# Three column tiles beside the arriving input, a fourth under the norm, and the shift from two more context columns

## Chip, cores and metric

One core of a Trainium2 chip runs the whole kernel. The metric is device time in microseconds (us) from start to end of one execution; several executions were timed, and one more was taken with the profiler. Engines: PE multiplies matrices, PEld loads its weights, DVE, ACT and POOL work on elements, SP issues most of the DMAs.

## What is computed

The kernel is one layer of a diffusion backbone over 1024 latent tokens of width 1024, with 256 context tokens in front. Cut to what matters here:

```python
u_lat = _modulate(_rmsnorm(x, norm1_g[l]), sh1, sc1)        # x*(1+scale)+shift
u_ctx = _modulate(_rmsnorm(ctx, norm1_g[l]), csh1, csc1)
rgx_l, rgg_l, mlx_l, mlo_l, gr_l, gm_l = jnp.split(u_lat @ w_in, splits, axis=-1)
rgx_c, rgg_c, mlx_c, mlo_c, gr_c, gm_c = jnp.split(u_ctx @ w_in, splits, axis=-1)
...
xm_l, q_l, k_l, v_l, gin_l = _mlstm_inputs(_to_col_major(mlx_l, rows), ml_conv_w, ml_conv_b, ml_wq, ml_wk, ml_wv)
...
y_lat = _merge(y_rg_l, y_ml_l, gr_l, gm_l, w_branch_rg, w_branch_ml, w_out)
x = x + g1 * y_lat
h = _modulate(_rmsnorm(x, norm2_g[l]), sh2, sc2)
x = x + g2 * _swiglu(h, w_ffn_in[l], w_ffn_out[l])
```

The scales and shifts are products of a small vector with `w_mod`. The change touches the norm, the modulation, and the first column tiles of `u @ w_in` (those of `mlx`, numbers 16 to 23 of `w_in`). It rests on this: with x, the norm's factor r per token, the scale a per channel and the shift s per channel, `(x*a*r + s) @ W` is `r * ((x*a) @ W) + s @ W`. So a tile can be multiplied before r is known; its output is multiplied by r afterwards, and one number per output channel, the shift term `s @ W`, is added.

## The kernel before

**Numbers in two halves.** Each operand of a matmul is a rounded high half and a low half (the rest). `load_split` (L89) loads a tile of weights (128x1024) into `wr`, POOL makes the high half `wh` (L94), DVE the low half `wl` (L97). `gemm` (L104) runs three products per 128-deep step k, each as a pair of 512-wide matmuls: high by high (L110), low of the input by high (L112), high by low of the weights (L114). One column tile against one k is called a part: six matmuls. A tile is eight parts.

**The beginning** (L338 to L454) is written out by hand: PE, ACT, DVE and POOL take their instructions in the order of the text. The input comes in eight pieces x[k]; a wmod pair (`mod_a` L276, `mod_b` L288) gives the scale of two pieces: PE forms `psmod`, ACT copies it to `mo`, PE sums it with `sel` to `psm`, DVE adds it into `modc` and `a1`. `un_h` (L315) is ACT's scaled copy, the high half of the input without the norm; `un_lo` (L319) DVE's low half; `un_sq` (L322) ACT's square, summed on DVE for the norm. `part(k, (0, 1))` multiplies tiles 16 and 17 with piece k; the scaled copy of piece k+1 stands ahead of part k in the text.

**The norm.** `rms_cols` (L140) sums the squares over the partitions (`prms`) and takes the root, `bcast_col` (L148) spreads the result over the partitions through PE (`rbl`), ACT copies it to `rb`. Meanwhile the last shift products (`mod_a`, `mod_b` of 0 to 3) and the shift term are formed: `psh` (L411), 16 products of a whole weight tile with one column. Then x is loaded again, `normed` (L328) and `normed_low` (L333) write the real modulated input into `uh` and `ul` in the order KB, beginning with piece 5, and tiles 18 and 19 are multiplied piece by piece with it. Beside this ACT squares the context pieces and POOL sums them (L307), and POOL multiplies the outputs X of tiles 16 and 17 by `rb` (L445).

**The stage behind it** (pool `p1`, L458 on, ordered by the scheduler) forms small matrices (`small_mats` L476), and for each of the eight tiles the context columns (`context` L495, 256 wide), for tiles 20 to 23 the latent ones (`latent` L490), then a convolution, a tanh and the small products `pv` and `pgt`. Then come an RG-LRU part whose first gate matmuls are `pt` (L700), and the mLSTM: `gate_out(4)` (L806) multiplies four column tiles of the output gates, which need nothing of the mLSTM, and then `head` (L817) runs four times. Head 0 loads masks and G, its inputs `xa`, `vv` and two matrices of decay rows, `SW` and `Sb`, each in two directions, by SP's queue; its first matmul is `pq` (L842).

## Time and profile before

| | |
|---|---|
| median of three runs | 1912.44 us (1911.99 to 1913.51) |
| the profiled execution's own time | 1913.69 us |
| its span | 1911.9 us |
| mean granted clock of PE | 0.991 of full speed |
| PE busy | 1847.2 us, 97% of the span |
| DVE, ACT, POOL busy | 64%, 32%, 18% |
| chain of waits that ended last | PE 89%, DVE 6%, ACT, DMA, POOL and issue 1% each |

The rows below are of that execution; times in them are us from the start of its span. A row of a timeline gives the start, the duration (of all its instructions together), engine, line, operation, tiles and count, and in brackets how long the engine stood idle before it and what released it.

### The profile page before, as it was taken

What the parts mean: (1) busy time and instruction counts of PE and PEld (TensorE: products, weight loads), DVE (VectorE), ACT (ScalarE), POOL (GpSimd) and SP (SyncE); (2) the same over time, 40 slices, a digit from 0 to 9 for tenths busy, and PEclk for the clock granted to TensorE, in tenths of its full rate; (3) what the DMA queues carried; (4) which work ended last, traced back from release to release, by engine and by line L of the source; (5) the groups of instructions that cost most, each with busy time, mean ns of one, the idle gap of its engine ahead of it and who ended that gap; (6) DMA issues with size and microseconds to landing.
All of it is one profiled execution on the core that took longest, in us unless ns stands there. A gap on an engine that the chain in (4) does not pass through costs nothing.

```text
span 1911.9 us, 23058 instructions
## 1 busy us (share of the span) xinstructions
PE 1847.2 (97%) x8878; PEld 1520.5 (80%) x8878; DVE 1230.9 (64%) x1887; ACT 610.0 (32%) x842; POOL 348.0 (18%) x452
## 2 busy tenths in 40 slices
PE   6799999999999999999999999999999999999997
PEld 4678778888877878788888888778888888888886
DVE  4676558888716474747776446787755555587755
ACT  3433256767422222222310112443333333210013
POOL 0311111111116151515101013220000000110003
PEclk9899999999999999999999999999999999999998
DMA  9432211212260515150796444343322222653102
GB/s 269 153 141 114 91 53 51 65 50 68 100 187 21 166 25 163 26 162 13 253 346 236 145 150 140 105 143 133 132 85 86 78 83 100 222 176 107 56 1 88
DMA packets 89989, 228.83 MB, mean 120 GB/s; under 512 B 8056, under 2 KB 37272, under 8 KB 89752
## 3 DMA queue, kind: packets, MB, share of 16 engines
q1 hardware_dynamic: 77160, 183.28, 30.0%
q0 software_dynamic: 11888, 43.54, 5.9%
q8 instruction: 70, 1.15, 0.3%
q10 hardware_dynamic: 832, 0.53, 0.1%
q14 instruction: 39, 0.32, 0.1%
HBM read 177.42 MB, written 49.91 MB: 119 GB/s over the span
## 4 chain that ended last, share of the span: by engine, by line
PE 89%; DVE 6%; ACT 1%; DMA 1%; issue 1%; POOL 1%; SPq 0%; DVEq 0%; ACTq 0%
PE pg L110 11%; PE pg L112 11%; PE pg L114 11%; PE pp L1122 7%; PE pp L1124 7%; PE pp L1123 7%; PE pp L1334 4%; PE pp L1336 4%; PE pp L1335 4%; PE po L891 3%; PE pC L896 3%; PE po L889 2%; PE po L110 2%; PE po L112 2%; PE po L114 2%; DMA wm<-in_wmod 1%
## 5 line engine op out<-in xcount | busy, mean ns | idle before, releaser
L110 PE MATMUL pg<-ah,wh 128*128 128x512 f32 x896 | 284.6, 398 | 4.6 <-ACT X L222 3.5
L112 PE MATMUL pg<-al,wh 128*128 128x512 f32 x896 | 282.7, 396 | 5.4 <-DVE al L335 5.4
L114 PE MATMUL pg<-ah,wl 128*128 128x512 f32 x896 | 280.6, 394 | 1.6 <-DVE wl L97 1.6
L94 POOL TENSOR_SCALAR wh<-wr 128x1024 fp32r<-128x1024 f32 x102 | 114.3, 1124 | 597.2 <-PE pg L112 217.5
L97 DVE TENSOR_TENSOR wl<-wr,wh 128x1024 fp32r<-128x1024 f32 x102 | 126.6, 1243 | 120.1 <-POOL wh L94 119.5
L112 PEld LDWEIGHTS pg<-al,wh 128*128 128x128 f32 x896 | 165.4, 190 | 39.9 <-DVE al L335 6.2
L110 PEld LDWEIGHTS pg<-ah,wh 128*128 128x128 f32 x896 | 165.4, 191 | 37.9 <-issue 5.6
L114 PEld LDWEIGHTS pg<-ah,wl 128*128 128x128 f32 x896 | 165.7, 189 | 36.9 <-DVE wl L97 2.0
L1334 PE MATMUL pp<-hh,wh 128*128 128x512 f32 (+1 forms) x384 | 145.1, 378 | 0.0
L1336 PE MATMUL pp<-hh,wl 128*128 128x512 f32 (+1 forms) x384 | 144.8, 377 | 0.0
L1335 PE MATMUL pp<-hh,wh 128*128 128x512 f32 (+1 forms) x384 | 144.8, 377 | 0.0
L1348 DVE SCALAR_TENSOR_TENSOR xs<-pp,g,xs 128x512 f32<-128x512 f32 x144 | 105.3, 746 | 47.8 <-PE pp L1336 43.9
L1122 PE MATMUL pp<-th,oh 128*128 128x512 f32 x264 | 102.8, 389 | 0.0
L1124 PE MATMUL pp<-th,ol 128*128 128x512 f32 x264 | 102.7, 389 | 0.0
L1123 PE MATMUL pp<-tl,oh 128*128 128x512 f32 x264 | 102.7, 389 | 0.0
L1134 DVE TENSOR_TENSOR c<-c,pp 128x512 f32<-128x512 f32 x82 | 56.2, 685 | 69.7 <-PE pp L1124 53.0
L1163 ACT ACTIVATE oh<-os 128x512 fp32r<-128x512 f32 x88 | 55.4, 631 | 130.9 <-PE pp L1123 111.7
L1282 POOL DMA_DIRECT2D s_h<-c x44 | 24.0, 545 | 356.6 <-DVE c L1281 356.6
L1164 DVE TENSOR_TENSOR ol<-os,oh 128x512 fp32r<-128x512 f32 x88 | 60.5, 689 | 39.8 <-ACT oh L1163 39.8
L1334 PEld LDWEIGHTS pp<-hh,wh 128*128 128x128 f32 x384 | 73.1, 190 | 14.0
L1335 PEld LDWEIGHTS pp<-hh,wh 128*128 128x128 f32 x384 | 73.0, 190 | 14.1
L1336 PEld LDWEIGHTS pp<-hh,wl 128*128 128x128 f32 x384 | 73.0, 190 | 13.8
(337 smaller groups left out, 3811.8 us busy)
## 6 DMA issues: line engine op xcount, KB each, us to landing
wr<-in_wfi SPq DMA_DIRECT2D x52, 512.0 KB, 3.3
wr<-in_win SPq DMA_DIRECT2D x48, 512.0 KB, 3.4
wr<-in_wmt SPq DMA_DIRECT2D x32, 512.0 KB, 5.1
s_h<-c POOLq DMA_DIRECT2D x44, 256.0 KB, 2.6
wr<-in_wfo SPq DMA_DIRECT2D x22, 512.0 KB, 3.9
g<-s_h SPq DMA_DIRECT2D x22, 512.0 KB, 4.6
wm<-in_wmod SPq DMA_DIRECT2D x16, 512.0 KB, 6.8
wr<-in_wo SPq DMA_DIRECT2D x16, 512.0 KB, 3.5
```

The lines of the kernel that those rows point to most:

```text
L94: nc.gpsimd.tensor_scalar(h, r, 1.0, 0.0, op0=ALU.mult, op1=ALU.add)
L97: nc.vector.tensor_tensor(l, r, h.bitcast(F32), op=ALU.subtract)
L110: nc.tensor.matmul(o, lhsT=wh[:, k], rhs=h(k), start=f, stop=False)
L112: nc.tensor.matmul(o, lhsT=wh[:, k], rhs=l(k), start=False, stop=False)
L114: nc.tensor.matmul(o, lhsT=wl[:, k], rhs=h(k), start=False, stop=e)
L1122: nc.tensor.matmul(o, lhsT=wh(k), rhs=bh(k), start=new and k == 0, stop=False, skip_group_check=True)
L1123: nc.tensor.matmul(o, lhsT=wh(k), rhs=bl(k), start=False, stop=False, skip_group_check=True)
L1124: nc.tensor.matmul(o, lhsT=wl(k), rhs=bh(k), start=False, stop=not more and k == n - 1, skip_group_check=True)
L1334: nc.tensor.matmul(po, lhsT=wh[:, m], rhs=hh[:, sl], start=i == 0, stop=False)
L1335: nc.tensor.matmul(po, lhsT=wh[:, m], rhs=hl[:, sl], start=False, stop=False)
L1336: nc.tensor.matmul(po, lhsT=wl[:, m], rhs=hh[:, sl], start=False, stop=i == n - 1)
L1348: nc.vector.scalar_tensor_tensor(xs[:, m, sls[t]], po, g2[:, m:m + 1], xs[:, m, sls[t]], op0=ALU.mult, op1=ALU.add)
```

## The change

Tiles 16, 17 and 18 are multiplied without the norm while the input arrives, 24 parts in place of 16, and `un_h` of a piece stands right ahead of its own part. The second weight tile and the second input piece are loaded ahead of the second wmod pair. Tile 19 is multiplied without the norm too, from the same `uh` and `ul`, while the norm is formed. The loop with the norm then works on tiles 20 and 21. The 16 products `psh` are gone; the context operand gets two more columns that hold the latent shift, so the context matmuls of tiles 16 to 19 are 258 wide and yield the shift term. The four X are multiplied by `rb` on DVE behind the loop (two on POOL in the loop before). The context squares are summed with two wide squares and five POOL additions in place of eight and seven. In `p1` the contexts of six tiles come first, then the small matrices; only tiles 22 and 23 are left for the latent side there; and three of the four gate tiles that stood ahead of the first mLSTM head move into it (`side_early`). PSUM is divided anew, and the scratch for DMA descriptors of POOL's queue shrinks from its default to 4096 bytes.

```diff
+NU = 4
+CW = TC + 2
...
-    ch = uc.tile([128, KT, TC], F32R, name="ch")
-    cl = uc.tile([128, KT, TC], F32R, name="cl")
+    ch_ = uc.tile([128, KT, CW], F32R, name="ch")
+    cl_ = uc.tile([128, KT, CW], F32R, name="cl")
+    ch, cl = ch_[:, :, 0:TC], cl_[:, :, 0:TC]
...
+    xpp = tc.tile_pool(name="xp", bufs=4, reuse_waits="tile")
+    xp = xpp.__enter__()
+    with pool("p0g", bufs=3, space=PSUM) as pg_, pool("p0s", bufs=2, space=PSUM) as ps_:
...
             load_x(0)
-            wfirst = [load_split(win[16], wf_, "f", late=True)]
+            wfirst = [load_split(win[16 + m], wf_, "f", NU, late=True) for m in range(2)]
+            load_x(1)
             load_mod(10, 11)
-            load_x(1)
-            wfirst.append(load_split(win[17], wf_, "f", late=True))
+            wfirst.append(load_split(win[18], wf_, "f", NU, late=True))
...
+            def ctx_sums(j):
+
+                sq = accl.rearrange("p (a b) -> p a b", a=4)
+                nc.scalar.activation(accl, c_t[j].rearrange("p a b -> p (a b)"), AF.Square)
+                nc.gpsimd.tensor_tensor(accl[:, 0:512], accl[:, 0:512], accl[:, 512:1024], op=ALU.add)
+                if j:
+                    nc.gpsimd.tensor_tensor(accc, accc, sq[:, 0], op=ALU.add)
+                    nc.gpsimd.tensor_tensor(accc, accc, sq[:, 1], op=ALU.add)
+                else:
+                    nc.gpsimd.tensor_tensor(accc, sq[:, 0], sq[:, 1], op=ALU.add)
...
             def un_sq(k):
-                sq = accl if k == 0 else (rb, sqx)[k % 2]
+                sq = accl if k == 0 else X4[2 + k % 2][:, 0:T]
                 nc.scalar.activation(sq, x_sb[k], AF.Square)
...
+                first = range(NU - 1)
+                pgs = [pg_.tile([128, 2, 512], F32, tag="g", name="pg") for _ in first]
...
                 un_h(0)
                 wfirst[0][2]()
                 un_lo(0)
-                mod_a(10, 11)
-                load_mod(14, 15)
+                wfirst[1][2]()
+                part(0, (0, 1))
                 un_h(1)
                 un_lo(1)
-                wfirst[1][2]()
+                part(1, (0, 1))
+                mod_a(10, 11)
...
+                wfirst[2][2]()
+                part(0, (2,))
+                mod_b(10, 11)
...
+                part(7, first)
                 mod_b(4, 5, 6, 7)
-                yr = rms_cols(p0, pc_.tile([128, 512], F32, tag="c", name="prms"), accl, 8)
+                put_latent(X4[0], pgs[0])
+                pgs.append(pg_.tile([128, 2, 512], F32, tag="g", name="pg"))
+                yr = rms_cols(p0, ps_.tile([128, 512], F32, tag="s", name="prms"), accl, 8)
...
+                part(KB[0], (3,))
+                part(KB[1], (3,))
                 rbl = [ps_.tile([128, 512], F32, tag="s", name="rbl") for _ in range(2)]
                 for j in range(2):
                     for c in range(4):
                         bcast_col(p0, yr[:, 4 * j + c:4 * j + c + 1], rbl[j][:, c * 128:c * 128 + 128])
                     nc.scalar.activation(rb[:, sls[j]], rbl[j], AF.Copy)
+                    part(KB[2 + j], (3,))
+                wfirst += [load_split(win[16 + m], late=True) for m in (NU, NU + 1)]
...
+                for k in KB[4:]:
+                    part(k, (3,))
...
-                normed(5)
-                psh = ps_.tile([128, 512], F32, tag="s", name="psh")
-                for m in range(2):
-                    for kk in range(KT):
-                        nc.tensor.matmul(psh[:, m:m + 1], lhsT=wfirst[m][3][:, kk], rhs=modc[:, kk, 0:1], start=kk == 0, stop=kk == KT - 1)
-                normed_low(5)
...
                 for i, k in enumerate(KB):
...
-                    if i == 1:
-                        ctx_sums()
-                    if i == 0:
-                        nc.vector.tensor_copy(shw, psh[:, 0:2])
-                    part(k, (2, 3))
-                    if i == 3:
-                        yc = rms_cols(p0, pc_.tile([128, 512], F32, tag="c", name="prms"), accc, 2)
+                    if i in (1, 2):
+                        ctx_sums(i - 1)
+                    part(k, (NU, NU + 1))
+                    if i == 4:
+                        yc = rms_cols(p0, ps_.tile([128, 512], F32, tag="s", name="prms"), accc, 2)
                     if i == 6:
                         rbc = ps_.tile([128, 512], F32, tag="s", name="rbc")
                         for c in range(2):
                             bcast_col(p0, yc[:, c:c + 1], rbc[:, c * 128:c * 128 + 128])
-                    if i in (1, 3):
-                        m = (i - 1) // 2
...
+                sh2 = modc[:, 0:KT, 0:1].to_broadcast([128, KT, 2])
+                nc.scalar.activation(ch_[:, :, TC:CW], sh2, AF.Identity)
+                nc.vector.tensor_tensor(cl_[:, :, TC:CW], sh2, ch_[:, :, TC:CW].bitcast(F32), op=ALU.subtract)
                 for k in range(KT):
                     nc.vector.scalar_tensor_tensor(c_sb[k], c_sb[k], a1[:, k, 1:2], rbc[:, 0:TC], op0=ALU.mult, op1=ALU.mult)
                     nc.scalar.activation(ch[:, k], c_sb[k], AF.Identity, bias=modc[:, k, 1:2])
-                for k in range(KT):
-                    nc.vector.scalar_tensor_tensor(cl[:, k], c_sb[k], modc[:, k, 1:2], ch[:, k].bitcast(F32), op0=ALU.add, op1=ALU.subtract)
-            pgs = pgs[2:]
-
+                    if k:
+                        nc.vector.scalar_tensor_tensor(cl[:, k - 1], c_sb[k - 1], modc[:, k - 1, 1:2], ch[:, k - 1].bitcast(F32),
+                                                       op0=ALU.add, op1=ALU.subtract)
+                k = KT - 1
+                nc.vector.scalar_tensor_tensor(cl[:, k], c_sb[k], modc[:, k, 1:2], ch[:, k].bitcast(F32), op0=ALU.add, op1=ALU.subtract)
+                for X in X4:
+                    xv = X[:, 261:1285].rearrange("p (w r) -> p w r", r=16)
+                    nc.vector.tensor_tensor(xv, xv, rb.rearrange("p (r w) -> p w r", r=16), op=ALU.mult)
...
+            def context(m, X):
+
+                n = CW if m < NU else TC
+                pc = ps_.tile([128, 512], F32, tag="s", name="pc")
+                gemm(wfirst[m], [(pc[:, 0:n], lambda k: ch_[:, k, 0:n], lambda k: cl_[:, k, 0:n])])
+                nc.scalar.activation(X[:, 2:258], pc[:, 0:TC], AF.Copy)
+                if m < NU:
+                    nc.vector.tensor_copy(shw[:, m:m + 1], pc[:, TC:TC + 1])
+                    nc.scalar.activation(X[:, 261:1285], X[:, 261:1285], AF.Identity, bias=shw[:, m:m + 1])
...
+            for m in range(NU):
+                context(m, X4[m])
+            wfp.__exit__(None, None, None)
...
+            def side_early():
+                j, m = sides.pop(0)
+                w = load_split(win[32 + 8 * j + m])
+                pg = pg_.tile([128, 2, 512], F32, tag="g", name="pg")
+                gemm(w, halves(pg, uh, ul))
+                t = wp.tile([128, KT, 128], F32, tag="wr", name="st", bufs=3).rearrange("p a b -> p (a b)")
+                nc.scalar.activation(t, pg.rearrange("p a b -> p (a b)"), AF.Tanh, scale=0.5)
+                nc.gpsimd.dma_start(s_g[j, m], t)
...
             small_mats()
             nc.gpsimd.dma_start(s_G, G)
...
-                    context(m + 1)
+                X = X4[m]
+                if m in (0, 2, 4):
+                    side_early()
+                if m in (4, 5):
+                    latent(m + 2)
...
-        gate_out(4)
+        gate_out(1)
...
-    nc = _bacc.Bacc("TRN2", target_bir_lowering=False, num_devices=1)
+    nc = _bacc.Bacc("TRN2", target_bir_lowering=False, num_devices=1, dynamic_dma_scratch_size=4096)
```

Two places in the order of the instructions. The first is ACT's queue around the third and fourth piece. Before (`ah` is the scaled copy into the high half, `sqx` and `rb` hold squares, `mo` is the copy of a modulation product):

```order
L317 ACTIVATE ah_91<-x_176,a1_73 128x1024
L324 ACTIVATE sqx_150<-x_169 128x1024
L285 ACTIVATE mo_298<-psmod_281 128x256
L317 ACTIVATE ah_91<-x_210,a1_73 128x1024
L324 ACTIVATE rb_152<-x_176 128x1024
L317 ACTIVATE ah_91<-x_212,a1_73 128x1024
```

With the change (`X_149`, `X_150` hold squares):

```order
L318 ACTIVATE ah_91<-x_180,a1_73 128x1024
L284 ACTIVATE mo_332<-psmod_315 128x256
L325 ACTIVATE X_149<-x_180 128x1024
L318 ACTIVATE ah_91<-x_215,a1_73 128x1024
L325 ACTIVATE X_150<-x_215 128x1024
L318 ACTIVATE ah_91<-x_217,a1_73 128x1024
```

Behind the copy of the modulation product the scaled copy came next, and the square after it; now the square comes next, and the scaled copy of piece 3 (`x_215`) after it.

The second place is PE's queue from the sums of the squares (`prms`) to the broadcast of the norm. Before (`pg` are the parts of tiles 16 and 17 with the last piece; `psh` the shift term):

```order
L143 MATMUL prms_476<-ones_70,accl_149 128x1 x8
L110 MATMUL pg_180<-ah_91,wh_162 128x512 x2
L112 MATMUL pg_180<-al_92,wh_162 128x512 x2
L114 MATMUL pg_180<-ah_91,wl_164 128x512 x2
L110 MATMUL pg_181<-ah_91,wh_173 128x512 x2
L112 MATMUL pg_181<-al_92,wh_173 128x512 x2
L114 MATMUL pg_181<-ah_91,wl_175 128x512 x2
L282 MATMUL psmod_516<-wm_431,s2_77 32x128 x8
```

and, after three more `psmod` rows and all but the last of eight `rbl` rows:

```order
L152 MATMUL rbl_556<-dg_579,ones_70 128x128
L292 MATMUL psm_583<-sel_69,mo_549 128x2 x4
L411 MATMUL psh_591<-modc_72,wr_160 128x1 x8
L411 MATMUL psh_591<-modc_72,wr_171 128x1 x8
L110 MATMUL pg_628<-ah_91,wh_366 128x512 x2
L112 MATMUL pg_628<-al_92,wh_366 128x512 x2
L114 MATMUL pg_628<-ah_91,wl_368 128x512 x2
```

With the change (`pg_544` is tile 19 without the norm):

```order
L145 MATMUL prms_545<-ones_70,accl_146 128x1 x8
L112 MATMUL pg_544<-ah_91,wh_418 128x512 x2
L114 MATMUL pg_544<-al_92,wh_418 128x512 x2
L116 MATMUL pg_544<-ah_91,wl_420 128x512 x2
L112 MATMUL pg_544<-ah_91,wh_418 128x512 x2
L114 MATMUL pg_544<-al_92,wh_418 128x512 x2
L116 MATMUL pg_544<-ah_91,wl_420 128x512 x2
L154 MATMUL rbl_580<-dg_582,ones_70 128x128
```

and, after two more `rbl` rows:

```order
L154 MATMUL rbl_580<-dg_591,ones_70 128x128
L112 MATMUL pg_544<-ah_91,wh_418 128x512 x2
L114 MATMUL pg_544<-al_92,wh_418 128x512 x2
L116 MATMUL pg_544<-ah_91,wl_420 128x512 x2
L154 MATMUL rbl_581<-dg_601,ones_70 128x128
```

Parts of a tile that needs no norm now stand between `prms` and the `rbl`, and between the two groups of `rbl`; `psh` is gone, and the products for the shift (`psmod`) stand behind the broadcast.

## Rows read from the trace of the kernel before

**Rows 1.** The page, busy time by engine and its share of the span

```profile
PE 1847.2 (97%) x8878; PEld 1520.5 (80%) x8878; DVE 1230.9 (64%) x1887; ACT 610.0 (32%) x842; POOL 348.0 (18%) x452
```

**Rows 2.** Stages: from:to, length, busy PE, PEld, DVE, ACT, POOL (instructions); PEclk, DMA share, GB/s

```profile
23.45:59.81 36.36, 34.64 (x257) 27.14 (x257) 22.80 (x33) 17.01 (x20) 3.47 (x12) 0.95 0.82 300
59.81:72.10 12.29, 8.43 (x121) 8.12 (x121) 6.05 (x10) 5.37 (x8) 0.00 (x0) 0.87 0.57 189
72.10:105.44 33.34, 27.43 (x105) 21.52 (x105) 25.33 (x30) 15.00 (x24) 14.06 (x9) 0.84 0.22 68
254.64:262.00 7.36, 6.33 (x23) 5.10 (x24) 1.48 (x1) 3.95 (x3) 0.00 (x0) 0.77 0.00 0
```

**Rows 3.** Timeline of PE, 19 to 30 us: start, us, line, operation, count, idle before

```profile
19.73 1.08 PE L282 MATMUL psmod<-wm,s 128*32 128x128 f32 x16 [10.13 <-DMA wm<-in_wmod]
...
25.30 1.05 PE L114 MATMUL pg<-ah,wl 128*128 128x512 f32 x2
26.16 1.05 PE L110 MATMUL pg<-ah,wh 128*128 128x512 f32 x2
...
29.27 0.63 PE L114 MATMUL pg<-ah,wl 128*128 128x512 f32 x2
29.74 0.63 PE L110 MATMUL pg<-ah,wh 128*128 128x512 f32 x2
```

**Rows 4.** Timeline of DVE: first low half of weights; a low half of the input

```profile
19.36 1.23 DVE L97 TENSOR_TENSOR wl<-wr,wh 128x1024 fp32r<-128x1024 f32 x1 [9.37 <-POOL wh L94]
...
44.78 1.28 DVE L320 SCALAR_TENSOR_TENSOR al<-x,a,ah 128x1024 fp32r<-128x1024 f32 x1
```

**Rows 5.** Timeline of ACT: copy of a modulation product, square, scaled copy

```profile
39.67 0.38 ACT L285 ACTIVATE mo<-psmod 128x256 f32<-128x256 f32 x1 [1.91 <-PE psmod L282]
39.95 1.05 ACT L324 ACTIVATE sqx<-x 128x1024 f32<-128x1024 f32 x1
40.90 1.14 ACT L317 ACTIVATE ah<-x,a 128x1024 fp32r<-128x1024 f32 x1
```

**Rows 6.** Timeline of PE, 53 to 96 us

```profile
53.50 2.04 PE L143 MATMUL prms<-ones,accl 128*128 128x1 f32 x16
...
64.89 3.70 PE L411 MATMUL psh<-modc,wr 128*128 128x1 f32 x32 [0.35 <-DVE modc L293]
72.10 1.19 PE L110 MATMUL pg<-ah,wh 128*128 128x512 f32 x2 [3.51 <-ACT X L222]
...
95.01 1.22 PE L112 MATMUL pg<-al,wh 128*128 128x512 f32 x2 [5.38 <-DVE al L335]
```

**Rows 7.** Timeline of POOL, 77 to 93 us

```profile
77.61 7.76 POOL L307 TENSOR_TENSOR accc<-accc,sqc 128x256 f32<-128x256 f32 x7 [18.28 <-ACT sqc L306]
```

**Rows 8.** Groups of DVE lines in the mLSTM: a multiplication through a permuted view

```profile
L954 DVE SCALAR_TENSOR_TENSOR t<-t,y 128x1024 f32<-128x1024 f32 x8 | 15.7, 1960 | 0.2
```

**Rows 9.** Timeline of PE around the first gate matmul

```profile
254.64 0.50 PE L700 MATMUL pt<-xh,rh 128*128 128x512 f32 x1 [2.42 <-ACT xh L666]
256.17 0.50 PE L701 MATMUL pt<-X,rh 128*128 128x512 f32 x1 [1.03 <-DVE X L670]
```

**Rows 10.** Timeline of ACT before it

```profile
245.11 0.39 ACT L657 ACTIVATE X<-pc 128x256 f32<-128x256 f32 x1 [4.04 <-PE pc L114]
```

**Rows 11.** Timeline of SP, loads of the first head

```profile
511.61 0.42 SPq L814 DMA_DIRECT2D masks<-in_masks  x1
...
524.90 1.13 SPq L821 DMA_DIRECT2D xa<-s_xm  x2
...
535.39 4.15 SPq L831 DMA_DIRECT2D SW<-s_row  x1
```

**Rows 12.** Timeline of DVE, masks onto the second decay matrix

```profile
549.81 2.15 DVE L853 TENSOR_TENSOR SW<-SW,masks 128x512 f32<-128x512 f32 x2 [6.93 <-DMA SW<-s_row]
```

**Rows 13.** Timeline of ACT, exponentials of the second decay matrix

```profile
550.53 3.04 ACT L855 ACTIVATE SW<-SW,cols 128x128 f32<-128x128 f32 x10 [4.84 <-DVE SW L853]
```

**Rows 14.** Timeline of PE, first matmul of the first head

```profile
574.13 3.60 PE L842 MATMUL pq<-xa,G 128*128 128x512 f32 x8
```

More of the change, by code (lines that the diff above doesn't have):

```diff
@@ L193, in conv_pads @@
         nc.gpsimd.memset(X[:, 1285:1287], 0.0)
+    sides = [(j, m) for j in range(2) for m in range(KT)]
     uh, ul = act_pool()
@@ L338, in hybrid_block @@
             with tc.manual_schedule(engines=ENG4):
-                pgs = [pg_.tile([128, 2, 512], F32, tag="g", name="pg") for _ in range(2)]
+                first = range(NU - 1)
+                pgs = [pg_.tile([128, 2, 512], F32, tag="g", name="pg") for _ in first]
                 mod_a(8, 9)
@@ L637, in side_store @@
         nc.gpsimd.dma_start(s_g[j, m], side_tanh(pg, t))
-    sides = [(j, m) for j in range(2) for m in range(KT)]
     with pool("p2") as p2, pool("p2c", bufs=1, space=PSUM) as pc_:
```

147 lines of the change are left out of this document (64 added, 83 removed).

## Prediction

> **What bounds the kernel now.** I read the page first: TensorE (PE) is busy 97% of the span [rows 1]. So time can only come from work that PE no longer does, from stretches in which it stands idle, and from stretches at half clock. The change takes almost no work from PE: the 16 products `psh`, 3.70 us [rows 6], and it adds two columns to four context tiles. What it can win is in the idle and slow stretches, so next I read the windows by stage [rows 2]: while the input arrives PE is busy 34.64 of 36.36 us, with the clock at 0.95; in the norm's stage 8.43 of 12.29 us, and none of that is tile work; in the first loop with the norm 27.43 of 33.34 us at 0.84. Then the timeline tells which waits these are: 10.13 us for wmod at the start [rows 3], 3.51 us before the loop and 5.38 us inside it [rows 6], and, later, 2.42 and 1.03 us at the first gate matmul [rows 9].
>
> Prices. Two pairs of matmuls start 0.86 us apart at 25.30 and 0.47 us apart at 29.27 [rows 3]: the half and the full level of the clock. A part has three pairs, so 1.41 us at full clock and 2.58 at half, and a tile of eight parts takes 11.3 us. What a stall costs beyond itself I take from [rows 2], 254.64 to 262.00: the mean clock is 0.77 after the stall of 2.42 us, so 0.23 of 7.36, or 1.7 us, is lost.
>
> The sum goes by five stages; each is compared for the same work of PE, so where the new kernel has done a tile more, 11.3 us are added to the old one.
>
> **A, to the end of the third tile and the sums of squares.** Before: 59.81, and 11.3 for the third tile, 71.1 us. With the change the first pair need not wait for the second wmod pair. The high half of the first weights is there at about 19.4 (its low half begins at 19.36 [rows 4]), 4 us before the old first part at 23.45. From there: 24 parts, 33.8 us; products with wmod, three sets of two at some 1.0 us and one of four at 2.0 (a set took 1.08 at half clock [rows 3]), 5.0 us; the sums with `sel` and `prms` (2.04 at half clock [rows 6]), about 3.9 us as an estimate. Now the waits. The change drops the lead of one piece: the scaled copy of piece 3 stands on ACT behind the copy of the modulation product, which waits for PE, and behind a square. When PE has done that product it therefore waits 0.38 + 1.05 + 1.14 us for the three ACT instructions [rows 5], and after one pair for the rest of the low half on DVE (1.28 us [rows 4] less 0.47): 3.1 us with some overlap taken off. The same pattern is at piece 5. At piece 4 the scale itself comes late, 2.4 us; at piece 2 about 1.0; at piece 0 the low half of the weights and then of the input, 1.23 + 1.28 us less the pairs that run, 1.5. Together 11.1 us, an estimate from walking the queues with these durations. Start at half clock: 1.3 us. Two waits (pieces 3 and 5) are as long as the stall of 2.42, so two more slow stretches, 3.4 us. Sum 19.4 + 33.8 + 5.0 + 3.9 + 11.1 + 1.3 + 3.4 = 77.9, so **+6.8** (+3.5 with no slow stretches, +7.5 if each wait is a little longer).
>
> **B, norm and the loop with the norm.** Before, 59.81 to 105.44: 45.6 us for two tiles, and 11.3 for a third, 56.9. With the change three tiles at full clock take 33.9 us; `rbl` about 1.9, the shift's `psmod` and `psm` 2.7, the sums for the context 1.0, some slow clock behind `prms` 1.4, and waits of 4.6 remain (estimates; the loop still alternates between DVE's two operations and PE). Sum 45.5, **-11.4** (-13 to -9). The low clock, the wait of 3.51 and `psh` go because tile 19 needs nothing of the norm; what covers the norm's chain is its eight parts, 11.3 us against the 12.29 us of the old stage. Without that cover the waits of 3.51 and 5.38 us would be back.
>
> **C, contexts first.** Context 0 now follows the loop at once, paced by two DVE operations per piece that are a quarter as wide as a low half, 0.4 us each as an estimate: 6.4 us for eight pieces against some 3 us of matmuls. Small matrices, which stood there before, no longer fill this. DVE has four multiplications of X ahead of the convolutions, each between 1.28 [rows 4] and 1.96 us [rows 8], where POOL had two. POOL's sums shrink from seven additions (7.76 us [rows 7]) to five, two of them twice as wide, about as long; it was off the path and stays there. **+3** (+2 to +8, the upper end if DVE's four also hold the first convolution up).
>
> **D, before the first gate matmul.** Between the last copy of a context at 245.11 [rows 10] and the first gate matmul at 254.64 [rows 9] lies a chain of copy, convolution and rounding of 9.5 us, and PE ran dry 2.42 us before its end, then waited 1.03 more. In the new order 15 rows of tile work stand there in place of 8: seven more pairs, 3.3 us. That fills the first stall, leaves about 0.7 of both, and the slow stretch of 1.7 goes: **-4.4** (-2 if the slow stretch stays).
>
> **E, the first mLSTM head.** Three gate tiles, 33.9 us, leave their place ahead of head 0 (they fill `p1` instead, where they cost the same). So `pq` comes at 574.13 [rows 14] less 33.9, 540.2. It needs `xa` and G; what follows it, `pS`, needs ACT's copy of it, behind the exponentials of the second decay matrix. Those end 3.7 us after the matrix has landed: 549.81 [rows 12] to 553.6 [rows 13]. Today the landing is 24 us early, afterwards it would be late if nothing else moved. But in SP's queue the load of weights ahead of `xa` is gone, so `xa` may issue soon after the masks (511.61) rather than at 524.90 [rows 11], and with it the second `SW`, which issues at 535.39 and lands 14.4 us later: at about 523 and 537.5. The exponentials then end at 541.2, when `pq` still runs. I take **+1** (0 to +8 where the loads start later).
>
> Sum: 6.8 - 11.4 + 3 - 4.4 + 1 = **-5.0 us**. Against the profiled execution, 1913.69, this is 1908.7; the median of the runs is 1.25 us lower, so I predict the new median at 1912.44 - 5.0 = **1907.4 us**. The bounds of all five terms added give -12 to +12; they won't all fall one way.
>
> **A rule against the change.** The trace shows that PE came back at the low level after the idle 2.42 us [rows 2, 9]. The Trainium skill (TensorE: Matmul & The Clock Gate, Part 1: The HAM clock gate) calls low the default state, which activity releases and idleness brings back; its section on oscillation describes a kernel whose every wait costs the clock again. The trace agrees for this stall. By that rule the many short waits of A, where the old kernel had one piece of lead, would each start slow; that is the first rival, priced from the rows.
>
> **Rivals.**
> 1. The clock falls at the smaller waits too: piece 2, piece 4 and the start of the new loop. Three more stretches at 1.7 us take back 5.1 us: 1912.5, no change. For it: the old loop's clock is 0.84 with waits of 3.51 and 5.38. Against: these waits are shorter, and PE works between them.
> 2. Slower: the first head stands uncovered. If the second `SW` lands as late as now, at 549.8, because its buffers come free no earlier, the exponentials end at 553.6, the copy of `pq` at 554.6, and `pS` waits from 543.8 to 554.7: 10.9 us and a slow stretch of 1.7, in place of the 1 in the sum: -5.0 + 11.6 = +6.6, 1919.0. It decides from a landing at about 540; from there each us costs one, and at about 545 the gain is gone. For it: 33.9 us of cover go, and these loads are chained through one queue. Against: the queue's weight load that held them is gone.
> 3. The change doesn't do what it says: the second weight tile and the second piece, moved ahead of wmod, arrive no sooner than before. The DMAs work at a share of 0.82 in that stage [rows 2], so the order of arrival decides, and if the parts begin at the old 23.45 rather than 19.4, 4 us of A are lost: 1911.4, no change.
>
> **How the numbers follow.** A difference below 0.2%, 3.8 us, can't be told from none. The forecast has 0.58 (its lower half and most of its upper one lie beyond 3.8 us faster: 0.50 faster, 0.08 same), rival 1 0.15 (same 0.12, faster 0.03), rival 3 0.11 (same 0.07, faster 0.04), rival 2 0.16 (slower 0.15, same 0.01). So faster 0.57, same 0.28, slower 0.15. The range: down to -12, all bounds at their good ends, 1900.4; up to 1914.5, which holds rivals 1 and 3 and leaves out the greater part of rival 2.
>
> **What would show it.** Right: parts begin near 19.4 us; waits on `ah` from ACT of 2 to 3 us at pieces 3 and 5, with low clock behind them; `prms` ends near 78; no wait of 3.5 or 5.4 us between the norm and the loop; no stall above 1 us at the first gate matmul, and none on `pS` in the first head. Wrong: waits in A that sum to over 15 us, a stall of PE on the exponentials of head 0, or idle time at the first contexts above 8 us.

## Result and profile after

| | before | with the change |
|---|---|---|
| median of six runs | 1912.01 us | 1925.31 us |
| lowest to highest | 1909.18 to 1913.51 | 1920.34 to 1928.69 |
| ratio | | 1.0069, 95% interval 1.0057 to 1.0081 |
| span of the profiled execution | 1911.9 us | 1925.0 us |

The change makes the kernel slower by 0.7%, some 13 us; 5 us faster were forecast. The page of the changed kernel, against [rows 1]:

```profile
PE 1852.5 (96%) x8846; PEld 1524.0 (79%) x8846; DVE 1232.6 (64%) x1895; ACT 611.5 (32%) x839; POOL 343.9 (18%) x448
```

PE is busy 5.3 us longer than before, although `psh` (3.70 us [rows 6]) is gone; so some 9 us come from the same work at a lower clock (the mean granted clock went from 0.991 to 0.986). In the rest of the span it stands idle: 72.5 us, where it was 64.7. The windows by stage (the columns are those of [rows 2]), cut at the end of the sums of squares, of the loop with the norm, at the first gate matmul and at the first matmul of the first head:

```profile
18.22:82.98 64.76, 52.80 (x340) 40.12 (x341) 25.32 (x26) 19.59 (x22) 8.26 (x16) 0.92 0.59 216
82.98:129.52 46.54, 42.07 (x242) 32.75 (x241) 31.76 (x48) 18.43 (x25) 8.65 (x8) 0.96 0.18 59
129.52:303.18 173.66, 161.20 (x921) 133.20 (x921) 107.31 (x158) 49.37 (x76) 24.57 (x44) 0.92 0.33 119
303.18:585.07 281.89, 281.73 (x1353) 235.76 (x1352) 221.50 (x162) 176.36 (x155) 33.04 (x58) 1.00 0.25 78
585.07:1925.00 1339.93, 1311.52 (x5961) 1080.02 (x5959) 844.10 (x1486) 342.92 (x555) 266.57 (x314) 0.99 0.37 124
```

and two windows of the kernel before that stand for the third and the fourth:

```profile
105.44:254.64 149.20, 142.88 (x873) 115.28 (x872) 97.20 (x148) 43.45 (x72) 22.12 (x46) 1.00 0.32 118
254.64:574.13 319.49, 316.70 (x1495) 263.95 (x1495) 227.07 (x165) 182.17 (x164) 38.39 (x64) 0.99 0.26 82
```

To compare them, tiles that the one kernel has done and the other has not are added, at about 11.0 us each (24 pairs 0.46 us apart):

| end of | before | changed | difference |
|---|---|---|---|
| sums of squares, 3 tiles done | 59.81 + 11.0 = 70.8 | 82.98 | +12.2 |
| loop with the norm, 6 tiles done | 105.44 + 22.0 = 127.4 | 129.52 | +2.1 |
| first gate matmul, 3 gate tiles more | 254.64 + 33.0 = 287.6 | 303.18 | +15.5 |
| first matmul of the first head | 574.13 | 585.07 | +10.9 |
| the span | 1911.9 | 1925.0 | +13.1 |

The stages so give +12.2, -10.1, +13.4, -4.6 and +2.2. **The loss is made in two places**: while the input arrives, and between the loop and the first gate matmul. Of the +13.4, 6.1 us are more idle time (12.5 us in place of 6.3), and 7.3 us are work that took longer.

The first place, PE's timeline with the change:

```profile
18.22 1.22 PE L112 MATMUL pg<-ah,wh 128*128 128x512 f32 x2 [8.62 <-POOL wh L96]
21.45 1.22 PE L114 MATMUL pg<-al,wh 128*128 128x512 f32 x2 [2.01 <-DVE al L321]
...
42.81 0.73 PE L112 MATMUL pg<-ah,wh 128*128 128x512 f32 x2 [2.54 <-ACT ah L318]
44.23 1.22 PE L114 MATMUL pg<-al,wh 128*128 128x512 f32 x2 [0.69 <-DVE al L321]
...
46.11 1.05 PE L112 MATMUL pg<-ah,wh 128*128 128x512 f32 x2
...
51.68 0.73 PE L112 MATMUL pg<-ah,wh 128*128 128x512 f32 x2 [1.63 <-ACT ah L318]
53.61 0.73 PE L114 MATMUL pg<-al,wh 128*128 128x512 f32 x2 [1.20 <-DVE al L321]
...
54.90 1.06 PE L112 MATMUL pg<-ah,wh 128*128 128x512 f32 x2
...
62.65 0.73 PE L112 MATMUL pg<-ah,wh 128*128 128x512 f32 x2 [2.48 <-ACT ah L318]
64.07 0.83 PE L114 MATMUL pg<-al,wh 128*128 128x512 f32 x2 [0.69 <-DVE al L321]
64.70 1.05 PE L116 MATMUL pg<-ah,wl 128*128 128x512 f32 x2
```

The parts begin at 18.22 us, earlier than forecast. At pieces 3, 4 and 5 PE waits 3.2, 2.8 and 3.2 us for the scaled copy and then the low half. The first pair behind a wait still takes 0.73 us; of those that follow, some take 1.05 us, as at 46.11, 54.90 and 64.70: half clock.

The second place, first the start of the contexts, PE:

```profile
134.57 0.58 PE L112 MATMUL pc<-ch,wh 128*128 128x258 f32 x1 [4.90 <-ACT X L220]
...
159.33 0.41 PE L515 MATMUL psG<-wi,qk 128*128 128x32 f32 x2 [1.29 <-DVE wi L510]
```

then ACT, where L220 empties tiles 20 and 21, two instructions each:

```profile
133.28 1.24 ACT L220 ACTIVATE X<-pg 128x512 f32<-128x512 f32 x2
141.65 0.70 ACT L220 ACTIVATE X<-pg 128x512 f32<-128x512 f32 x1 [7.13 <-issue]
...
142.77 0.38 ACT L491 ACTIVATE X<-pc 128x256 f32<-128x256 f32 x1
```

and DVE:

```profile
133.81 7.68 DVE L463 TENSOR_TENSOR X<-X,rb 128x1024 f32<-128x1024 f32 x4
...
144.57 0.95 DVE L188 TENSOR_SCALAR cy<-X,vt 128x1284 f32<-128x1284 f32 x1 [1.22 <-ACT X L494]
```

PE does nothing for 4.90 us ahead of the first context, then runs it at half clock. ACT empties tile 20 at 133.28, behind the eight context pieces; that is what PE waits for. It waits 7.13 us more to empty tile 21 (named "issue"), until DVE's four multiplications end at 141.5, and the copy of the first context (142.77) is behind that. The first convolution (L188) begins at 144.57. Four stretches with their clock: those from 134.57, 160.20 and 224.92 follow waits of PE and are slow, the one that ends at 160.20 is not:

```profile
134.57:139.47 4.90, 4.89 (x23) 4.90 (x23) 4.90 (x4) 0.00 (x0) 0.00 (x0) 0.50 0.00 0
155.32:160.20 4.88, 3.58 (x27) 3.19 (x27) 4.84 (x5) 0.30 (x2) 0.00 (x0) 0.99 0.54 220
160.20:177.13 16.93, 16.93 (x61) 15.10 (x61) 8.21 (x29) 1.27 (x1) 1.68 (x3) 0.50 0.15 59
224.92:228.00 3.08, 3.08 (x7) 2.46 (x8) 1.08 (x1) 0.00 (x0) 0.00 (x0) 0.51 0.79 267
```

and the small matrices in the kernel before, with a wait of PE among them:

```profile
115.76:128.95 13.19, 12.11 (x103) 11.74 (x101) 6.29 (x26) 2.83 (x3) 1.65 (x2) 1.00 0.25 91
```

```profile
118.73 0.50 PE L110 MATMUL pg<-ah,wh 128*128 128x512 f32 x1 [1.08 <-POOL wh L94]
```

From 160.20 to 177.13 PE is busy all the time and runs at 1.2 GHz: until 172.3 these are most of the small matrices with some tile work between them, then 4.8 us of tile work alone. They stand just behind a wait of 1.29 us for the scaling `wi` on DVE (159.33 above). Before, the small matrices ran at full clock, although PE had waited 1.08 us among them; and in the changed kernel a wait of 1.33 us for a low half of weights, at 209.47, is followed by full clock. So the length of a wait alone does not tell whether a slow stretch follows.

### The profile page after: what moved, and what is told of

Its sections match the earlier page's. It is cut to its first block, busy times and chain, and to the rows that moved or that the text cites. A ratio compares the mean times of both kernels' runs of the same rounds, so it can differ in the third digit from the quotient of the medians.

```text
span 1925.0 us, 22977 instructions
## 1 busy us (share of the span) xinstructions
PE 1852.5 (96%) x8846; PEld 1524.0 (79%) x8846; DVE 1232.6 (64%) x1895; ACT 611.5 (32%) x839; POOL 343.9 (18%) x448
## 3 DMA queue, kind: packets, MB, share of 16 engines
q0 software_dynamic: 11888, 43.54, 5.9%
## 4 chain that ended last, share of the span: by engine, by line
PE 88%; DVE 6%; ACT 2%; issue 2%; DMA 1%; POOL 1%; SPq 0%; ACTq 0%; DVEq 0%; POOLq 0%
PE pg L114 12%; PE pg L116 12%; PE pg L112 12%; PE pp L1154 7%; PE pp L1155 7%; PE pp L1156 7%; PE pp L1366 4%; PE pp L1367 4%; PE pp L1368 4%; PE po L923 3%; PE pC L928 3%; PE po L921 2%; PE po L112 2%; PE po L114 2%; PE po L116 1%
## 5 line engine op out<-in xcount | busy, mean ns | idle before, releaser
L112 PE MATMUL pg<-ah,wh 128*128 128x512 f32 x896 | 289.0, 402 | 19.4 <-POOL wh L96 11.7
L114 PE MATMUL pg<-al,wh 128*128 128x512 f32 x896 | 285.7, 399 | 6.8 <-DVE al L321 5.2
L112 PEld LDWEIGHTS pg<-ah,wh 128*128 128x128 f32 x896 | 166.3, 192 | 54.6 <-POOL wh L96 12.2
L114 PEld LDWEIGHTS pg<-al,wh 128*128 128x128 f32 x896 | 166.8, 192 | 43.9 <-DVE al L321 7.6
L99 DVE TENSOR_TENSOR wl<-wr,wh 128x1024 fp32r<-128x1024 f32 x102 | 127.4, 1251 | 100.5 <-POOL wh L96 100.4
```

The lines of the kernel that those rows point to most:

```text
L99: nc.vector.tensor_tensor(l, r, h.bitcast(F32), op=ALU.subtract)
L112: nc.tensor.matmul(o, lhsT=wh[:, k], rhs=h(k), start=f, stop=False)
L114: nc.tensor.matmul(o, lhsT=wh[:, k], rhs=l(k), start=False, stop=False)
```

## Experiments

Each run was timed beside the kernel before on the same chip; ratios are to it, the change itself is at 1.0069 (1.0057 to 1.0081), and differences from the change are taken from the ratios. All are edits of the changed kernel; where a run takes together edits of runs before it, its heading names them. Line numbers are a few off.

**1. Lead restored.**

```diff
                 un_lo(2)
+                un_h(3)
+                un_lo(3)
                 part(2, first)
...
-                un_h(3)
-                un_lo(3)
-                part(3, first)
+                part(3, first[:1])
                 mod_b(12, 13)
+                un_h(4)
+                un_lo(4)
+                part(3, first[1:])
...
-                un_h(4)
-                un_lo(4)
+                un_h(5)
+                un_lo(5)
                 part(4, first)
...
-                un_h(5)
-                un_lo(5)
                 part(5, first[:1])
```

> The scaled copies of pieces 3, 4 and 5 and the modulation sums for 4 and 5 are placed one part earlier, so that the copy leads its part by a piece again; the work is the same. Theory (A: the lost lead costs the waits of 2.5+0.7, 1.6+1.2 and 2.5+0.7 us and three slow stretches of about 1.5 us): sums of squares end 10 to 14 us earlier, gain of the whole kernel 8 to 14 us. Rival (the arrival of the input sets the pace): the waits turn into waits for DMA, gain below 3 us.

Measured: 1908.16 us, ratio 0.9969 (0.9956 to 0.9982), some 19 us below the change and faster than the kernel before. PE:

```profile
34.43 0.73 PE L114 MATMUL pg<-al,wh 128*128 128x512 f32 x2 [0.59 <-DVE al L321]
...
45.06 0.73 PE L114 MATMUL pg<-al,wh 128*128 128x512 f32 x2 [0.32 <-DVE al L321]
...
56.12 0.74 PE L114 MATMUL pg<-al,wh 128*128 128x512 f32 x2 [0.58 <-DVE al L321]
...
68.83 0.71 PE L112 MATMUL pg<-ah,wh 128*128 128x512 f32 x2
```

PE no longer waits at pieces 3 and 5, and 0.32 us at piece 4 (45.06); the waits at 34.43 and 56.12 are at pieces 2 and 6. The sums of squares end at 68.83 rather than 82.98, 14.2 us earlier, the upper end of what was expected. No part waits for a DMA, so the rival falls. The whole gain is larger than the 8 to 14 us expected: some 5 us more come behind the loop, where the small matrices happened to run nearer to full clock (0.82 from 146.50 to 156.00). The edit did not aim at that part.

**2. Scaling of the gate weights on POOL.**

```diff
-                nc.vector.tensor_scalar(wi[:, 1], wi[:, 1], 1.0 / 16.0, None, op0=ALU.mult)
+                nc.gpsimd.tensor_scalar(wi[:, 1], wi[:, 1], 1.0 / 16.0, None, op0=ALU.mult)
```

> The scaling of the small gate weights by 1/16 moves from DVE, where it stands behind a convolution, to POOL. Theory a (the stall of 1.3 us on this scaling lets the clock fall, and small matrices keep it low for 17 us): the stall goes, the small matrices run at full clock as in the kernel before, gain 7 to 10 us. Rival b (the small matrices by themselves bring the clock down in this order, stall or not): gain 1 to 2 us, granted clock still near 0.5 from 160 to 177 us. Rival c (DVE bound): no gain.

Measured: 1919.63 us, ratio 1.0037 (1.0024 to 1.0051), 6 us below the change; the wait is 0.94 us and the clock over the small matrices 0.86. Between a and b: a shorter stall, less slow clock, neither gone.

**3. The two PSUM pools change places.**

```diff
-    with pool("p1g", bufs=2, space=PSUM) as pg_, pool("p1s", bufs=4, space=PSUM) as ps_:
+    with pool("p1s", bufs=4, space=PSUM) as ps_, pool("p1g", bufs=2, space=PSUM) as pg_:
```

> The two PSUM pools of the stage behind the norm change places, so that the first context tile gets a bank that the loop no longer uses; nothing else is edited. Theory (the new wait of 4.9 us ahead of the first context is the bank of the sixth column tile, which ACT empties only behind the eight context pieces): the wait shrinks below 1.5 us, the contexts follow the pace of DVE (0.8 us per piece), the half clock behind the wait goes, and the whole kernel gains 4 to 7 us against the change. Rival (the stage is set by DVE, which now has four multiplications of X and the convolutions): PE starts the contexts earlier but waits as much later, gain below 1.5 us.

Measured: 1937.14 us, ratio 1.0121 (1.0104 to 1.0138), 10 us slower than the change: a miss on both accounts. The first context did start without a wait, at 132.4, but the second waited 8.20 us for the emptying of tile 21. And the scheduler put PE's rows in another order further on: the tile work that stood ahead of the small product `pend` is no longer there, and PE ran dry before it for 7.56 us (0.76 with the change).

**4. Lead, scaling and pools together** (the diffs of 1, 2 and 3).

> All three edits together. Theory: the three gains add, 19 to 31 us against the change, which is 6 to 18 us below the kernel before. Rival (a later stage, DVE or the loads of the first head, takes the gain back): less than half of the sum of the three single gains.

Measured: 1931.59 us, ratio 1.0100 (1.0085 to 1.0115). The same waits of 8.19 and 7.56 us are in it; the pools' loss swallowed the rest, and the run says nothing on whether gains add.

**5. The multiplications back on POOL.**

```diff
+                    if i >= 4:
+                        xv = X4[i - 4][:, 261:1285].rearrange("p (w r) -> p w r", r=16)
+                        nc.gpsimd.tensor_tensor(xv, xv, rb.rearrange("p (r w) -> p w r", r=16), op=ALU.mult)
...
-                    nc.vector.tensor_tensor(xv, xv, rb.rearrange("p (r w) -> p w r", r=16), op=ALU.mult)
```

> The four multiplications of X by rb go back from DVE to POOL, into the second half of the loop, as two of them were in the kernel before; the rest is the change. Theory (they hold rb until 141.5 us, ACT's emptying of the sixth tile waits 7 us for its place, and the context copies, the first convolution and the scaling of the small gate weights queue behind it): the first convolution starts 3 to 5 us earlier, the stall ahead of the small matrices goes, and with it their slow clock; gain 6 to 11 us. The wait of 4.9 us ahead of the first context stays. Rival (DVE slows down beside POOL, as a low half took longer beside POOL's sums before, and the contexts come later): gain below 2 us.

Measured: 1929.87 us, ratio 1.0102 (1.0087 to 1.0117), 6 us slower than the change, where 6 to 11 us faster was expected. DVE (the small operations of the context's norm), then POOL:

```profile
120.12 0.17 DVE L135 RECIPROCAL ry<-ru 128x2 f32<-128x2 f32 x1 [0.27 <-ACT ru L134]
120.32 1.53 DVE L136 TENSOR_TENSOR ru<-ry 128x2 f32<-128x2 f32 x1
121.88 2.84 DVE L137 TENSOR_TENSOR ru<-ru,rmsv 128x2 f32<-128x2 f32 x1
124.75 2.78 DVE L138 TENSOR_SCALAR ru<-ru 128x2 f32<-128x2 f32 x1
127.57 2.77 DVE L139 TENSOR_TENSOR ry<-ry,ru 128x2 f32<-128x2 f32 x1
```

```profile
118.96 11.36 POOL L448 TENSOR_TENSOR X<-X,rb 128x1024 f32<-128x1024 f32 x4
```

Operations on 128x2 elements take up to 2.8 us instead of 0.17: from 120.32 on, each ends when one of POOL's four multiplications does (11.36 us for four is 2.84 each, from 118.96), and DVE runs freely again at 130.3, when POOL is done. The RECIPROCAL in front of them kept its 0.17 us while POOL multiplied. PE then waits 8.22 us for the low half behind them. This is the wait of 5.38 us of [rows 6] seen from its cause. The same lines of the kernel before, DVE and POOL:

```profile
87.09 2.26 DVE L134 TENSOR_TENSOR ru<-ry 128x2 f32<-128x2 f32 x1
89.39 2.77 DVE L135 TENSOR_TENSOR ru<-ru,rmsv 128x2 f32<-128x2 f32 x1
```

```profile
85.33 6.82 POOL L445 TENSOR_TENSOR X<-X,rb 128x1024 f32<-128x1024 f32 x2
```

There two multiplications held the same chain until 92.2, 4.7 of the 5.38 us. So taking them from POOL was a gain of the change that the prediction had not seen, and put down to the order of the norm.

**6. Stores of the early gate tiles from ACT's queue.**

```diff
-                nc.gpsimd.dma_start(s_g[j, m], t)
+                nc.scalar.dma_start(s_g[j, m], t)
```

> The stores of the three early gate tiles are issued from ACT's queue instead of POOL's, where they wait for ACT's tanh ahead of the next high half of weights. Theory: the waits of 3.1 us on a high half near 223 us and of 0.9 us on its low half go, with the slow stretch behind them; gain 3 to 6 us. Rival (the high half waits for something else, its load or its buffer): same wait under another name, gain below 1 us.

Measured: 1922.99 us, ratio 1.0067 (1.0047 to 1.0086), as the change. The wait became 2.73 us: in POOL's queue the high half then stood behind another store,

```profile
217.65 0.53 POOL L554 DMA_DIRECT2D s_xm<-xm  x1 [7.84 <-DVE xm L553]
218.20 2.06 POOL L96 TENSOR_SCALAR wh<-wr 128x1024 fp32r<-128x1024 f32 x2
```

which waits for DVE's convolution. The rival was right for this edit.

**7. Gate tiles back ahead of the head.**

```diff
-                if m in (0, 2, 4):
-                    side_early()
...
-        gate_out(1)
+        gate_out(4)
```

> One part of the change undone: the four gate tiles stand ahead of the first mLSTM head again, and none in the stage behind the norm. Theory (the move itself fills the stall ahead of the first gate matmul and does no harm at the first head): the waits of 2.4 and 1.0 us there come back, 4 to 5 us slower than the change less 4 to 6 us for the stores that no longer hold POOL: within 3 us of the change, unless the small matrices, now without tile work between them, let the clock fall further (then slower by 3 to 10 us). Rival (the early tiles are what costs: their loads, high halves and stores crowd the stage): faster than the change by more than 6 us.

Measured: 1931.93 us, ratio 1.0113 (1.0098 to 1.0129), 8 us slower than the change, where within 3 us was expected. The waits at the first gate matmul are back, larger (4.05 and 1.03 us), and 2.47 us more stand ahead of them, for ACT at 261.29; the clock over the small matrices did not fall further (0.74 from 161.73 to 175.00). The move of the gate tiles earns its place.

**8. Five edits: lead, scaling, multiplications on POOL, stores on ACT, one bank passed over.**

> The lead restored, the small scaling on POOL, the four multiplications on POOL, the stores on ACT's queue, and one PSUM bank passed over (by a one-column write of ACT that nothing reads), so that the first context does not take the bank of the fifth tile. Theory: the wait of 4.9 us ahead of the contexts and its slow clock (some 5 us together) go as well; with 17 us of the lead's run and the other two, 27 to 36 us against the change, 1890 to 1899 us. Rival: the gains overlap, since the lead's run already had the small matrices at nearly full clock: 20 to 27 us, 1899 to 1906 us.

Measured: 1909.45 us, ratio 1.0006 (0.9985 to 1.0026), some 12 us below the change, where 27 to 36 or 20 to 27 were expected: it contains the harm of experiment 5, a wait of 8.21 us. Its ten executions lie between 1905.03 and 1921.87 us.

**9. Two places in memory.** From here the multiplications stay on DVE.

```diff
-            rb = p0.tile([128, T], F32, name="rb")
...
+            rb = p0.tile([128, T], F32, name="rb")
             with tc.manual_schedule(engines=ENG4):
...
+            skip = ps_.tile([128, 512], F32, tag="s", name="skip")
+            nc.scalar.activation(skip[:, 0:1], ones[:, 0:1], AF.Copy)
             for m in range(NU):
                 context(m, X4[m])
```

> Two edits of places in memory, none of the work: rb lies elsewhere in SBUF, so that the sixth tile's X no longer takes its place and ACT need not wait for DVE's four multiplications; and one PSUM bank is passed over (by a one-column write of ACT that nothing reads), so that the first context does not take the bank of the fifth tile. Theory (the first contexts wait for a bank, ACT for a place): no wait of 4.9 us, the first context follows DVE's 0.8 us per piece and ends 4 to 6 us earlier, ACT's wait of 7 us goes; gain 5 to 9 us. Rival (DVE's convolutions set the stage behind): the contexts come earlier, but PE waits as long at the small matrices; gain below 2 us.

Measured: 1919.57 us, ratio 1.0055 (1.0040 to 1.0070), some 3 us below the change, but the two intervals overlap. The 4.90 us are gone (the first context runs at 129.94), and ACT empties tile 21 at 134.80 without its wait. But the first convolution comes only 1.2 us earlier than with the change. ACT, then DVE:

```profile
142.22 1.16 ACT L494 ACTIVATE X<-X,shw 128x1024 f32<-128x1024 f32 x1 [5.80 <-DVE shw L493]
```

```profile
134.22 7.89 DVE L463 TENSOR_TENSOR X<-X,rb 128x1024 f32<-128x1024 f32 x4
...
143.41 0.95 DVE L188 TENSOR_SCALAR cy<-X,vt 128x1284 f32<-128x1284 f32 x1 [1.22 <-ACT X L494]
```

The first X still needs its shift, and DVE copies that (L493) only behind its four multiplications, at 142.02. So the four multiplications hold up the first convolution, and the place in SBUF does not. PE waits again a little later:

```profile
152.75 0.49 PE L515 MATMUL psG<-qk 128*128 128x128 f32 x2 [1.72 <-DVE shw L493]
154.20 1.22 PE L515 MATMUL psG<-qk 128*128 128x128 f32 x4 [0.96 <-ACT X L491]
```

The small matrices need the banks of the contexts, which DVE and ACT empty behind the convolution, and behind these waits they run slow again. Between theory and rival: the first wait was the bank (the run cannot part the two edits, but in experiment 3, with the place unchanged, the first context did not wait either), and DVE takes most of the gain back.

**10. Lead, scaling and the two places** (the diffs of 1, 2 and 9).

> The lead restored and the small scaling on POOL (the two single edits that gained), with the two edits of places in memory; the multiplications stay on DVE. Theory (the stages add, since each gain lies in a wait of PE of its own): 5 to 9 us below the run with the lead alone (1908.2), so 1899 to 1904 us, 0.4 to 0.7% below the kernel before. Rival (what is gained ahead of the convolutions is lost at them): within 2 us of the run with the lead alone.

Measured: 1906.78 us, ratio 0.9989 (0.9980 to 0.9999). By its ratio it is not below the lead alone (0.9969) but some 4 us above, with intervals that barely touch; so the theory fails, and the rival's "within 2 us" is missed on the other side. The waits of 1.90 and 0.96 us stand ahead of the small matrices as in 9, and the clock over them is 0.64. Behind them PE waits for a high half of weights, which POOL makes behind two stores:

```profile
200.91 1.22 PE L112 MATMUL pg<-ah,wh 128*128 128x512 f32 x2 [3.07 <-POOL wh L96]
```

```profile
196.31 0.53 POOL L557 DMA_DIRECT2D s_xm<-xm  x1 [10.66 <-DVE xm L556]
199.24 0.53 POOL L541 DMA_DIRECT2D s_g<-st  x1 [2.39 <-ACT st L540]
199.79 2.07 POOL L96 TENSOR_SCALAR wh<-wr 128x1024 fp32r<-128x1024 f32 x2
```

**11. The same, with the last tiles' weights loaded earlier.**

```diff
             def latent(m):
-                wfirst.append(load_split(win[16 + m]))
...
+                if m in (3, 5):
+                    wfirst.append(load_split(win[16 + 6 + m // 4]))
```

> As the run before it, with the weights of the last two column tiles loaded and split one step earlier in the text. Theory (the wait of 3 us on a high half comes from POOL's queue, where it stands behind a store that waits for a convolution): that wait and the 0.9 us behind it go, with a slow stretch; 3 to 5 us below the run before it. Rival (the three buffers for raw weights, shared with the early gate tiles, hold the load back): same wait, no gain.

Measured: 1898.52 us, ratio 0.9947 (0.9931 to 0.9964), 8 us below run 10, where 3 to 5 were expected. The waits of 3.07 and 1.33 us on the halves of weights are gone, and the slow stretch behind them; POOL makes the high half at 183.04, ahead of both stores. So it was the place in POOL's queue, and the buffers did not hold the load back.

**12. A whole gate tile ahead of the small matrices, on the change alone.**

```diff
+            side_early()
             small_mats()
...
-                if m in (0, 2, 4):
+                if m in (2, 4):
```

> One edit on the change: the first early gate tile stands ahead of the small matrices in the text, so that PE multiplies the whole tile first and the eight sets of small matrices follow it in one piece. Theory (the small matrices run at half clock because PE stands just before them, 1.3 us, for DVE, ACT or POOL, and their few columns then don't bring the clock back): without a stall ahead of them they run at full clock as in the kernel before; the stall and some 8 us of slow clock go, gain 6 to 10 us. Rival (they bring the clock down by themselves): granted clock near 0.5 in them again, gain below 3 us.

Measured: 1924.73 us, ratio 1.0076 (1.0048 to 1.0105), no gain. A wait of 1.28 us for DVE's copies came up inside the small matrices, at 170.74, and the clock fell. Four of the eight sets stand ahead of that wait and four behind it:

```profile
165.81:169.46 3.65, 3.65 (x33) 3.54 (x31) 3.60 (x2) 1.02 (x1) 1.59 (x2) 1.00 0.47 191
170.74:177.59 6.85, 6.85 (x32) 6.85 (x33) 2.59 (x18) 0.85 (x1) 0.00 (x0) 0.50 0.21 79
```

The same work takes 3.65 us at full clock and 6.85 at half, in one execution.

**13. The same on top of run 11.**

> The same edit on top of the run with all edits and the early weights (1898.5). Theory: the waits of 1.9 and 1.0 us ahead of the small matrices and their 14 us at half clock go, gain 6 to 10 us against that run, 1888 to 1893 us, about 1% below the kernel before. Rival: the clock falls in them again, gain below 3 us.

Measured: 1898.37 us, ratio 0.9953 (0.9937 to 0.9970), the same as run 11. This run separates clock and stall. All eight sets, and a new wait ahead of them:

```profile
152.99:160.20 7.21, 7.21 (x66) 7.21 (x65) 4.83 (x23) 2.30 (x2) 1.59 (x2) 1.00 0.34 124
```

```profile
141.30 1.22 PE L116 MATMUL pg<-ah,wl 128*128 128x512 f32 x2 [4.75 <-DVE wl L99]
```

The eight sets run without a break in 7.2 us at full clock, so they do not bring it down by themselves. The gain went to a new wait: 4.75 us at 141.30 for the low half of the gate tile, on DVE behind the first convolution, and a slow stretch after it (clock 0.57 from 141.00 to 145.00).

## Why the prediction was wrong, step by step

Two of its five terms failed: C above all, and the clock in A. B came out near its number partly by luck, D and E held. None of the three signs of being wrong that it named came up: the waits in A sum to 11.8 us (over 15 was the sign), PE is idle 4.90 us at the first contexts (over 8), and nothing waits for the exponentials of head 0.

**A, the lost lead: mechanism right, size too small.** The waits were forecast at 11.1 us; they measure 11.8 (2.01, 0.58, 2.54 + 0.69, 1.63 + 1.20, 2.48 + 0.69). What failed most is the term "1.3 + 3.4" for the clock. Pairs at half clock stand from 21.45 to 26.74 and behind all three waits, 44.23 to 47, 54.2 to 57.5 and 64.1 to 67.3: about 15 us, which costs some 7.5. From its first pair the stage was forecast at 58.5 us and took 64.8; the waits and the clock explain 3.5 of these 6.3 us, the rest is not assigned. Rival 1 had the clock at piece 4 (at piece 2 it did not fall), but priced it against no change. Run 1 shows that the lead is worth 14 us.

**B: the number right, -10.1 against -11.4, the reason only half.** The waits in the loop sum to 4.5 us (4.6 were forecast), each under 1 us except 1.94 for POOL's sums of the context, which the prediction had off the path. But the prediction has it that the wait of 5.38 us would be back without the eight parts of tile 19 as cover. Run 5 keeps that cover and has a wait of 8.22 us: the 5.38 us of the old loop were mostly POOL's two multiplications holding DVE's small operations. That the change took them from POOL anyway is the lucky part.

**C: the step that failed.** "+3 (+2 to +8)" measures, with the wait of 2.42 us that D had taken away already, +13.4, so about +16 by itself. I priced the contexts by DVE's pace alone. What came instead:
- a PSUM bank that ACT empties too late (4.90 us, then half clock); run 9 removes that wait by memory alone;
- DVE's four multiplications, which hold up the first convolution; the prediction named this, as the upper end of its bounds. The place in SBUF that rb holds made ACT wait 7.13 us, but run 9 removes that wait and the convolution comes only 1.2 us earlier;
- small matrices behind a DVE queue that now holds multiplications and convolutions: 1.29 us of wait and 17 us at half clock;
- POOL's high half behind a store that waits for a convolution and one that waits for a gate tile's tanh (3.07 us, then half clock); run 11 removes it.

The bank, the small matrices and POOL's queue were not in the sum, since I listed the work that moved, but not which buffer, bank or queue place each step inherits.

**D: right.** No wait is left at the first gate matmul, and the stage behind it gains 4.6 us. The old trace has there, besides the 1.03 us and the slow stretch, a wait of 1.57 us at 553 us (L114, for a low half) that the prediction did not count. One reading of it is not exact: PE did not come back at the low level after the 2.42 us. The granted clock is 1.00 from 254.64 to 256.00, and the slow matmuls begin at 256.5.

**E: right in substance, wrong in its times.** No wait arose at the first head, and rival 2 did not come. But "`pq` at 540.2" was wrong: the tiles moved ahead of the RG-LRU stage shift that stage and the loads of the head by the same 33 us, so `pq` was due near 574 again, and with the loss ahead of it came at 585.07. Only the distance between loads and `pq` shrank, and `xa` did issue right behind G, at 557.97. The second `SW` was masked at 583.49, just in time.

**Rival 3** did not happen: the parts began at 18.22.

**The last +2.2 us** lie mainly in a wait of 1.25 us at 965 us for ACT's tanh (L667), which the old trace does not have; what brought it was not tested.

Of the sign: slower had 0.15, by another mechanism. New waits with a slow stretch behind each are what rival 1 describes, but it looked for them only in A and at the start of the loop, three of them at 1.7 us, and so came out at "no change". No rival had them behind the loop.

**Left open.** What decides whether a slow stretch follows a short wait, and how long it lasts, no run here separates; executions of run 12 lie between 1914.37 and 1926.21 us, with mean clocks of 0.991 and 0.985. That DVE's queue sets the stage now is argued from the waits of runs 9, 12 and 13, and not shown by an experiment that takes work from DVE without giving it to POOL. The smaller scratch for POOL's DMA descriptors was not tested by itself; the pages show the same bytes in that queue before and after (43.54 MB).

## What to carry to other kernels

When a stage is rewritten, list for each moved step not only its work but what it inherits: the bank, the buffer and the place in a queue, and who empties them; four of the new waits here were of that kind, and three of them went with edits of memory or order alone (runs 9 and 11). One of the three, ACT's, gained next to nothing, since another wait stood right behind it. A scaled copy that leads its part by one piece costs no work and was worth 14 us: 8.3 us of waits, and most of the rest is the half clock behind them. With the lead, the scaling on POOL, the two places in memory and the earlier loads, the change is 0.5% faster than the kernel before (run 11, 1898.52 us, ratio 0.9931 to 0.9964), so the idea held, and what lost was the placing.

## What was not expected of the hardware

Tiny DVE operations (128x2) stood still while a 2.84 us POOL multiplication with a permuted view ran, and took 2.8 us each in place of 0.17 (run 5). DVE's operations on 1024 columns beside POOL's sums went from 1.28 to 1.75 or 2.3 us; what they lost, 0.5 to 1.0 us, is less than one of those sums takes (1.45 to 2.26 us). The Trainium skill (SBUF — State Buffer, SBUF: two separate sides) says that the two engines' common port pair is a lock held for a whole instruction, by whichever of a POOL operation and certain DVE operations starts first. Run 5 agrees: each of the small operations that were held ends with one multiplication, so its price is the other engine's duration and not its own size, and with a chain of four of them PE waited 8.2 us. And PE stayed at 1.2 GHz for 17 us while it was busy throughout, first with matmuls of 32 and 128 columns between those of 512, then with those of 512 alone. The eight sets of small matrices ran at 2.4 GHz in one piece in run 13, and in run 12 four of them did and four behind a wait of 1.28 us did not.
